# An RMS-norm kernel whose Tile context is closed after the first two loads, the rest in plain Bass

## The chip, the cores and the metric

The kernel runs on one core of one Trainium2 chip. The metric is the device time of one execution in microseconds (us). It is longer than the span, which reaches from the kernel's first instruction to its last: the difference holds what the runtime does behind the kernel. "Behind the span" means here the time minus the span. All runs quoted are at a granted clock of 1.0.

## The reference

```python
batch, seq, dim = 16, 1024, 512          # x is float32, gamma is all ones
rms = np.sqrt(np.mean(x ** 2, axis=-1, keepdims=True) + eps)
x_norm = x / rms * gamma
return np.maximum(x_norm, 0).astype(np.float32)
```

The input has 33.55 MB and so has the output; each is moved once.

## The kernel before

Each partition holds 16 rows of 512 numbers per chunk of 4 MB; eight chunks pass through six slots of SBUF. SyncE issues all loads and stores on one queue. ScalarE sums the squares of eight rows at a time and takes the root; VectorE inverts it, multiplies (by gamma too) and clips. GpSimd only waits for loads and passes them on as a count. The first chunk comes in two halves, so that compute starts early. All of it is traced inside a Tile context, in a critical section, with semaphores set by hand; the context adds its closing at the end.

```python
    ctx.enter_context(tc.manual_schedule(engines={mybir.EngineType.SP}))
    with tc.tile_critical():
        for m, (i, a, r) in enumerate(loads):        # loads of the first six chunks
            if i < nslots:
                load(m)                              # L77
        ...                                          # stores, the last two loads, and compute
    with nc.sync.register("landed") as landed:
        nc.sync.reg_mov(landed, 32)
        for s in range(nchunks - nslots, nslots):
            nc.sync.wait_ge(sem_slot[s], landed)
        nc.sync.reg_mov(landed, 64)
        for s in range(nchunks - nslots):
            nc.sync.wait_ge(sem_slot[s], landed)     # L171, the last wait
...
    with _tile.TileContext(nc) as tc:                # L202: on leaving it, Tile's closing
        tile_rmsnorm_relu_kernel(tc, *args)
```

## Time and profile before

| what | before |
|---|---|
| time, median of 4 runs | 162.28 us (162.23 to 162.32) |
| span of the profiled run | 160.37 us, its time 162.16 |
| transfers | first packet 1.95 us, last packet ends 158.84, last landing 159.32 |
| last wait passed | 159.34 us |
| Tile's closing | 159.40 to 160.37 us |
| behind the span | 162.16 - 160.37 = 1.79 us |

Read it in that order. The DMA row of the page, full to the last slice, says that the transfers bound the kernel. Everything that could be won is then ahead of the first packet or after the last one. The rows with L202 in the view of single source lines show the closing, which holds two barriers of all engines. The prediction below shows these lines.

### The profile page before, as it was taken

The numbers are of one execution on the slowest core, as the hardware profiler recorded it, in microseconds if no ns is written. First come the engines' busy times: TensorE is split into PE (matmuls) and PEld (weight loads), VectorE is DVE, ScalarE is ACT, GpSimd is POOL, SyncE is SP. The second block draws the span as 40 slices with busy tenths as digits, with TensorE's granted clock in tenths as the row PEclk, the third lists the DMA queues.
The fourth block names the chain that finished last, engine by engine and source line by source line (L and its number), as shares of the span: only waits on it lengthen the run. The fifth ranks groups of instructions, "written<-read, shape, count | busy, mean of one in ns | idle before, by whom it ended". The sixth has DMA issues, their size and how long they took to land. (4 is left out here: it accounts for less than half of the span.)

```text
span 160.4 us, 1008 instructions
## 1 busy us (share of the span) xinstructions
DVE 126.0 (79%) x164; ACT 86.3 (54%) x273; POOL 0.2 (0%) x4
## 2 busy tenths in 40 slices
DVE  1103989898989999999999999999999999995000
ACT  3088919889989988988910298899400000000000
POOL 0000000000000000000000000000000000000000
DMA  5999999999999999999999999999999999999993
GB/s 168 419 441 437 490 400 400 499 409 392 482 433 392 433 474 400 409 499 400 392 466 433 409 425 466 417 400 482 425 392 482 425 400 474 433 400 466 425 409 139
DMA packets 2456, 67.12 MB, mean 419 GB/s; under 512 B 276, under 2 KB 276, under 8 KB 280
## 3 DMA queue, kind: packets, MB, share of 16 engines
q1 hardware_dynamic: 2448, 67.11, 97.6%
q10 hardware_dynamic: 8, 0.01, 0.0%
HBM read 33.56 MB, written 33.55 MB: 419 GB/s over the span
## 5 line engine op out<-in xcount | busy, mean ns | idle before, releaser
L152 DVE SCALAR_TENSOR_TENSOR slots<-slots,rstd,gamma_sb 128x512 f32 x128 | 86.2, 747 | 4.8 <-DVEq L149 4.8
L128 ACT ACTIVATE junk<-slots 128x512 f32 x128 | 74.5, 582 | 22.2 <-ACTq L124 22.0
L163 DVE TENSOR_SCALAR slots<-slots x16 | 36.7, 2294 | 2.4 <-DVEq L162 0.2
L128 ACT ACTIVATION_READ_ACCUMULATOR junk<-slots x128 | 23.9, 187 | 0.0
L146 DVE RECIPROCAL rstd<-rms x16 | 3.2, 197 | 6.2 <-DVEq L142 6.2
L135 ACT ACTIVATE rms<-ss,eps_sb x16 | 4.8, 301 | 3.0 <-ACTq L134 3.0
L139 DVE LOAD_MASK_SELECT gamma_sb<-gseed x1 | 0.0, 14 | 6.0 <-DMA gseed<-in_gamma_dram 6.0
L120 ACT ACT_TABLE_LOAD x1 | 1.3, 1283 | 2.8 <-issue 2.8
L113 DVE MEMSET gseed<- 128x512 f32 x1 | 0.5, 485 | 1.1 <-SPq L93 1.1
L139 DVE STREAM_SHUFFLE gamma_sb<-gseed 128x512 f32<-128x512 f32 x1 | 0.7, 716 | 0.0
L188 POOL MEMSET const-bfloat16-1.0<- 128x1 bf16 x1 | 0.1, 102 | 0.0
L188 POOL MEMSET const-uint8-127<- 128x1 uint8 x1 | 0.1, 102 | 0.0
L188 POOL MEMSET const-float32-1.0<- 128x1 f32 x1 | 0.1, 99 | 0.0
L188 POOL MEMSET const-float32-0.0<- 128x1 f32 x1 | 0.1, 98 | 0.2 <-issue 0.2
L114 DVE MEMSET eps_sb<- 128x1 f32 x1 | 0.1, 59 | 0.0
## 6 DMA issues: line engine op xcount, KB each, us to landing
out_dram<-slots SPq DMA_DIRECT2D x8, 4096.0 KB, 20.7
slots<-in_x_dram SPq DMA_DIRECT2D x7, 4096.0 KB, 30.3
slots<-in_x_dram SPq DMA_DIRECT2D x2, 2048.0 KB, 9.6
gseed<-in_gamma_dram ACTq DMA_DIRECT2D x1, 8.0 KB
```

The costliest lines, as they stand in the source:

```text
L113: nc.vector.memset(gseed, 0.0).then_inc(sem_z, 1)
L114: nc.vector.memset(eps_sb, eps).then_inc(sem_z, 1)
L120: nc.scalar.preload_act_table(ACTF.Sqrt)
L128: a = nc.scalar.activation(out=junk[:, j, :], in_=slots[:, bass.ds(base + j * d, d)], func=ACTF.Square, accum_out=ss[:, bass.ds(col + j, 1)])
L135: nc.scalar.activation(out=rms[:, bass.ds(col, G)], in_=ss[:, bass.ds(col, G)], func=ACTF.Sqrt, bias=eps_sb, scale=inv_d).then_inc(sq, 1)
L139: nc.vector.stream_shuffle(gamma_sb, gseed, [0] * 32)
L146: nc.vector.reciprocal(out=rstd[:, bass.ds(col, G)], in_=rms[:, bass.ds(col, G)]).then_inc(sv, 1)
L152: r = nc.vector.scalar_tensor_tensor(out=row, in0=row, scalar=rstd[:, bass.ds(col + j, 1)], in1=gamma_sb, op0=ALU.mult, op1=ALU.mult)
L163: nc.vector.tensor_scalar_max(out=blk, in0=blk, scalar1=0.0).then_inc(done, 1)
L188: nc = _bacc.Bacc("TRN2", target_bir_lowering=False, num_devices=1)
```

## The change

The intent is to take Tile's closing out of the tail: Tile traces only the first two loads, is closed and compiled at once, and its closing barrier runs while these two transfer. All else follows as plain Bass. As Tile no longer clears the kernel's semaphores, each is brought back to zero by the engine that waits for it last.

```diff
-    with tc.tile_critical():
-        for m, (i, a, r) in enumerate(loads):
-            if i < nslots:
-                load(m)
+    early = 2
+    for m in range(early):
+        t = load(m)
+        tc.no_tile_sem_insts.add(t.ins.name)
+    ctx.close()
+    tc.close()
+    tc.compile()
+
+    for m, (i, a, r) in enumerate(loads):
+        if m >= early and i < nslots:
+            load(m)
     ...
+    def take(engine, sem, n):
+        engine.wait_ge(sem, n)
+        engine.sem_inc(sem, -n)
     ...
-    with nc.sync.register("landed") as landed:
-        nc.sync.reg_mov(landed, 32)
-        ...
+    take(nc.sync, done, ngroups)
+    take(nc.sync, tick1, ngroups)
+    take(nc.sync, tick3, ngroups)
+    for i in range(nchunks - nslots, nchunks):
+        take(nc.sync, sem_slot[i % nslots], 32 * (i // nslots + 1))
```

Cut from the diff: tensors and semaphores are now allocated from Bass instead of Tile, and the waits of the loops are written as takes. The loops themselves are the same.

More of the change, by code (lines that the diff above doesn't have):

```diff
@@ L40, with sbuf @@
     ov = out2.rearrange("(c p k) d -> c p k d", p=P, k=K)
-    singles = ctx.enter_context(tc.tile_pool(name="singles", bufs=1))
-    psum = ctx.enter_context(
-        tc.tile_pool(name="psum", bufs=1, space=bass.MemoryType.PSUM))
-    gseed = singles.tile([P, d], F32, name="gseed")
-    gamma_sb = singles.tile([P, d], F32, name="gamma_sb")
-    eps_sb = singles.tile([P, 1], F32, name="eps_sb")
-    ss = singles.tile([P, rows], F32, name="ss")
-    rms = singles.tile([P, rows], F32, name="rms")
-    rstd = singles.tile([P, rows], F32, name="rstd")
-    slots = singles.tile([P, nslots * K * d], F32, name="slots")
-    junk = psum.tile([P, G, d], F32, name="junk")
-    loads = [(0, 0, G), (0, G, K - G)] + [(i, 0, K) for i in range(1, nchunks)]
-    sem_half = tc.alloc_semaphore("half")
-    sem_slot = [tc.alloc_semaphore(f"slot{s}") for s in range(nslots)]
-    sem_g = tc.alloc_semaphore("gam")
-    sem_z = tc.alloc_semaphore("zero")
-    ready = tc.alloc_semaphore("ready")
-    sq = tc.alloc_semaphore("sq")
-    tick1 = tc.alloc_semaphore("tick1")
-    tick3 = tc.alloc_semaphore("tick3")
-    done = tc.alloc_semaphore("done")
-    sa = tc.alloc_semaphore("sa")
-    sv = tc.alloc_semaphore("sv")
+    def sbuf(name, shape):
+        return nc.alloc_sbuf_tensor(name, shape, F32).ap()
+    gseed = sbuf("gseed", [P, d])
+    gamma_sb = sbuf("gamma_sb", [P, d])
+    eps_sb = sbuf("eps_sb", [P, 1])
+    ss = sbuf("ss", [P, rows])
+    rms = sbuf("rms", [P, rows])
+    rstd = sbuf("rstd", [P, rows])
+    slots = sbuf("slots", [P, nslots * K * d])
+    junk = nc.alloc_psum_tensor("junk", [P, G, d], F32).ap()
+    loads = [(0, 0, G), (0, G, K - G)] + [(i, 0, K) for i in range(1, nchunks)]
+    sem_half = nc.alloc_semaphore("half")
+    sem_slot = [nc.alloc_semaphore(f"slot{s}") for s in range(nslots)]
+    sem_g = nc.alloc_semaphore("gam")
+    sem_z = nc.alloc_semaphore("zero")
+    ready = nc.alloc_semaphore("ready")
+    sq = nc.alloc_semaphore("sq")
+    tick1 = nc.alloc_semaphore("tick1")
+    tick3 = nc.alloc_semaphore("tick3")
+    done = nc.alloc_semaphore("done")
+    sa = nc.alloc_semaphore("sa")
+    sv = nc.alloc_semaphore("sv")
     def slot_ap(i):
@@ L76, in load @@
         i, a, r = loads[m]
-        nc.sync.dma_start(out=slot_ap(i)[:, a:a + r, :],
-                          in_=xv[i][:, a:a + r, :]
-                          ).then_inc(sem_half if m == 0 else sem_slot[i % nslots], 16)
-    def loaded(engine, m):
-        i = loads[m][0]
-        if m == 0:
-            engine.wait_ge(sem_half, 16)
-        else:
-            engine.wait_ge(sem_slot[i % nslots], 32 * (i // nslots) + 16)
+        return nc.sync.dma_start(out=slot_ap(i)[:, a:a + r, :],
+                                 in_=xv[i][:, a:a + r, :]
+                                 ).then_inc(sem_half if m == 0 else sem_slot[i % nslots], 16)
+    def take(engine, sem, n):
+        engine.wait_ge(sem, n)
+        engine.sem_inc(sem, -n)
     def store(i):
@@ L92 @@
     ctx.enter_context(tc.manual_schedule(engines={mybir.EngineType.SP}))
-    with tc.tile_critical():
-        for m, (i, a, r) in enumerate(loads):
-            if i < nslots:
-                load(m)
-        nc.sync.wait_ge(tick3, 6)
-        store(0)
-        store(1)
-        for s in range(2):
-            nc.sync.wait_ge(sem_slot[s], 32)
-            load(7 + s)
-        nc.sync.wait_ge(tick1, 11)
-        for i in range(2, nchunks):
-            store(i)
-        for m, (i, a, r) in enumerate(loads):
-            loaded(nc.gpsimd, m)
-            nc.gpsimd.sem_inc(ready, r // G)
-        nc.vector.memset(gseed, 0.0).then_inc(sem_z, 1)
-        nc.vector.memset(eps_sb, eps).then_inc(sem_z, 1)
-        nc.scalar.wait_ge(sem_z, 1)
-        nc.scalar.dma_start(out=gseed[0:P:32, :],
-                            in_=gamma[None, :].to_broadcast([P // 32, d])
-                            ).then_inc(sem_g, 16)
-        nc.scalar.preload_act_table(ACTF.Sqrt)
-        nc.scalar.wait_ge(sem_z, 2)
-        with nc.scalar.Fori(0, ngroups) as gi:
-            nc.scalar.wait_ge(ready, 1)
-            nc.scalar.sem_inc(ready, -1)
-            base = nc.scalar.snap((gi % (nslots * per)) * (G * d))
-            col = nc.scalar.snap(gi * G)
-            for j in range(G):
-                a = nc.scalar.activation(
-                    out=junk[:, j, :], in_=slots[:, bass.ds(base + j * d, d)],
-                    func=ACTF.Square, accum_out=ss[:, bass.ds(col + j, 1)])
-                if j == G - 1:
-                    a.then_inc(sa, 1)
-            nc.scalar.wait_ge(sa, 1)
-            nc.scalar.sem_inc(sa, -1)
-            nc.scalar.activation(out=rms[:, bass.ds(col, G)], in_=ss[:, bass.ds(col, G)],
-                                 func=ACTF.Sqrt, bias=eps_sb, scale=inv_d).then_inc(sq, 1)
-        nc.vector.wait_ge(sem_g, 16)
-        nc.vector.stream_shuffle(gamma_sb, gseed, [0] * 32)
-        with nc.vector.Fori(0, ngroups) as gi:
-            nc.vector.wait_ge(sq, 1)
-            nc.vector.sem_inc(sq, -1)
-            base = nc.vector.snap((gi % (nslots * per)) * (G * d))
-            col = nc.vector.snap(gi * G)
-            blk = slots[:, bass.ds(base, G * d)]
-            nc.vector.reciprocal(out=rstd[:, bass.ds(col, G)],
-                                 in_=rms[:, bass.ds(col, G)]).then_inc(sv, 1)
-            nc.vector.wait_ge(sv, 1)
-            nc.vector.sem_inc(sv, -1)
-            for j in range(G):
-                row = slots[:, bass.ds(base + j * d, d)]
-                r = nc.vector.scalar_tensor_tensor(
-                    out=row, in0=row, scalar=rstd[:, bass.ds(col + j, 1)], in1=gamma_sb,
-                    op0=ALU.mult, op1=ALU.mult)
-                if j == 0:
-                    r.then_inc(tick1, 1)
-                if j == 2:
-                    r.then_inc(tick3, 1)
-                if j == G - 1:
-                    r.then_inc(sv, 1)
-            nc.vector.wait_ge(sv, 1)
-            nc.vector.sem_inc(sv, -1)
-            nc.vector.tensor_scalar_max(out=blk, in0=blk, scalar1=0.0).then_inc(done, 1)
@@ L165 @@
-    with nc.sync.register("landed") as landed:
-        nc.sync.reg_mov(landed, 32)
-        for s in range(nchunks - nslots, nslots):
-            nc.sync.wait_ge(sem_slot[s], landed)
-        nc.sync.reg_mov(landed, 64)
-        for s in range(nchunks - nslots):
-            nc.sync.wait_ge(sem_slot[s], landed)
+    early = 2
[8 more added lines that the diff above has]
+            load(m)
@@ new lines @@
+    nc.sync.wait_ge(tick3, 6)
+    store(0)
+    store(1)
+    for s in range(2):
+        nc.sync.wait_ge(sem_slot[s], 32)
+        load(7 + s)
+    nc.sync.wait_ge(tick1, 11)
+    for i in range(2, nchunks):
+        store(i)
+    for m, (i, a, r) in enumerate(loads):
+        if m == 0:
+            take(nc.gpsimd, sem_half, 16)
+        else:
+            nc.gpsimd.wait_ge(sem_slot[i % nslots], 32 * (i // nslots) + 16)
+        nc.gpsimd.sem_inc(ready, r // G)
+    nc.vector.memset(gseed, 0.0).then_inc(sem_z, 1)
@@ new lines @@
+    nc.vector.memset(eps_sb, eps).then_inc(sem_z, 1)
+    nc.scalar.wait_ge(sem_z, 1)
+    nc.scalar.dma_start(out=gseed[0:P:32, :],
+                        in_=gamma[None, :].to_broadcast([P // 32, d])
+                        ).then_inc(sem_g, 16)
+    nc.scalar.preload_act_table(ACTF.Sqrt)
+    take(nc.scalar, sem_z, 2)
+    with nc.scalar.Fori(0, ngroups) as gi:
+        take(nc.scalar, ready, 1)
+        base = nc.scalar.snap((gi % (nslots * per)) * (G * d))
+        col = nc.scalar.snap(gi * G)
+        for j in range(G):
+            a = nc.scalar.activation(
+                out=junk[:, j, :], in_=slots[:, bass.ds(base + j * d, d)],
+                func=ACTF.Square, accum_out=ss[:, bass.ds(col + j, 1)])
+            if j == G - 1:
+                a.then_inc(sa, 1)
+        take(nc.scalar, sa, 1)
+        nc.scalar.activation(out=rms[:, bass.ds(col, G)], in_=ss[:, bass.ds(col, G)],
+                             func=ACTF.Sqrt, bias=eps_sb, scale=inv_d).then_inc(sq, 1)
@@ new lines @@
+    take(nc.vector, sem_g, 16)
+    nc.vector.stream_shuffle(gamma_sb, gseed, [0] * 32)
+    with nc.vector.Fori(0, ngroups) as gi:
+        take(nc.vector, sq, 1)
+        base = nc.vector.snap((gi % (nslots * per)) * (G * d))
+        col = nc.vector.snap(gi * G)
+        blk = slots[:, bass.ds(base, G * d)]
+        nc.vector.reciprocal(out=rstd[:, bass.ds(col, G)],
+                             in_=rms[:, bass.ds(col, G)]).then_inc(sv, 1)
+        take(nc.vector, sv, 1)
+        for j in range(G):
+            row = slots[:, bass.ds(base + j * d, d)]
+            r = nc.vector.scalar_tensor_tensor(
+                out=row, in0=row, scalar=rstd[:, bass.ds(col + j, 1)], in1=gamma_sb,
+                op0=ALU.mult, op1=ALU.mult)
+            if j == 0:
+                r.then_inc(tick1, 1)
+            if j == 2:
+                r.then_inc(tick3, 1)
+            if j == G - 1:
+                r.then_inc(sv, 1)
+        take(nc.vector, sv, 1)
+        nc.vector.tensor_scalar_max(out=blk, in0=blk, scalar1=0.0).then_inc(done, 1)
```

## The prediction

> **What bounds the kernel now.** I read the page first, then the DMA queue's own waits, the timeline of the last 30 us, the stretches at the end, and the single instructions by source line.
>
> The page says what is full:
>
> ```profile
> span 160.4 us, 1008 instructions
> DVE 126.0 (79%) x164; ACT 86.3 (54%) x273; POOL 0.2 (0%) x4
> DMA  5999999999999999999999999999999999999993
> ...
> q1 hardware_dynamic: 2448, 67.11, 97.6%
> ```
>
> No engine is full; the transfers are: one queue (q1) holds 16 engines for 97.6% of the span. The trace's packet records start at 1.95 us and end at 158.84 us, so 67.11 MB in 156.9 us, 428 GB/s without a hole. The kernel is therefore a head (before the first packet), a stream, and a tail (after the last packet). The chain view is of no help: it stops at VectorE's last operation at 144.2 us, as semaphore and DMA instructions are not counted as work.
>
> The waits of the DMA queue's own engine, SyncE, show what the end hangs on:
>
> ```profile
> SPq L77 <- DMA out_dram<-slots: 21.9, 2, 12.3
> SPq L171 <- DMA out_dram<-slots: 11.8, 1, 11.8
> ```
>
> L171 is the last wait of the kernel: SyncE stands there 11.8 us for the last stores. The stretches at the end and two source lines show what comes after it:
>
> ```profile
> 156.00:158.00 2.00, 0.00 (x0) 0.00 (x0) 0.00 (x0) 1.00 0.72 311
> 158.00:159.00 1.00, 0.00 (x0) 0.00 (x0) 0.00 (x0) 1.00 0.00 0
> 159.00:160.40 1.40, 0.00 (x0) 0.00 (x0) 0.00 (x0) 1.00 0.00 0
> ```
>
> ```profile
> L171 SPq EVENT_SEMAPHORE  x1: 17/17/17, 159.3 to 159.3; - x1
> ```
>
> ```profile
> L202 POOLq EVENT_SEMAPHORE  x4: 17/17/17, 159.6 to 160.3; - x4
> L202 SPq DRAIN  x3: 7/7/7, 159.5 to 159.9; - x3
> L202 SPq COMPARE_BRANCH  x2: 33/33/33, 0.8 to 159.4; - x2
> L202 POOLq EVENT_SEMAPHORE_RANGE_CLEAR  x1: 157/157/157, 159.9 to 159.9; - x1
> ```
>
> The columns of the stretches are length, busy time of three engines, clock, DMA share, GB/s. In the last stretch nothing moves. The source views (duration in ns, first and last start in us) say what runs there: the last wait passes at 159.34, then L202, the exit of Tile's context, runs a branch (159.40), a barrier of all engines (to 159.80), the clearing of Tile's range of semaphores (159.92, 157 ns) and a second barrier (160.19 to 160.37). That is 160.37 - 159.36 = **1.01 us** between the end of the last wait and the end of the span, on the path, with no work in it.
>
> **What the Trainium skill says.** (1) "DMA: Bandwidth & Descriptors", Specifications, gives a fabric ceiling of 435 GB/s for 16 engines. The trace agrees: 428 GB/s means that the stream has 2% left at most, and the change moves no byte. (2) "Perfetto Trace Analysis", Sequencer-only Instruction: the profiled window of such an instruction is its execution alone, the wait for a semaphore and its propagation are outside it. The trace agrees: the L171 entry lasts 17 ns but stood for 11.8 us. So I count the barrier by start times, not by durations. (3) "Runtime: NRT & Kernel Launch", The ~15us preamble/postamble breakdown: after the kernel the runtime makes a barrier over all engines, then resets semaphores. The trace agrees in kind: after the span a first series of nine updates of one semaphore runs from 160.61 to 161.13 us, the reset of all semaphores to 161.69, a second series from 161.92 to 162.27. The run timed 162.16 us against a span of 160.40, so about 1.8 us of the metric lies behind the span and is not the kernel's. (4) "DMA: Bandwidth & Descriptors", Queues, rings and completion order: each DMA engine takes turns between queues packet by packet, so gamma's small load has to queue beside the bulk. The trace agrees: gamma's issue ended at 2.73 us, its first packet began at 5.77 and it had landed at 7.54.
>
> **The change part by part.**
>
> *Removed at the end.* Tile's exit, its two barriers and the clearing no longer follow the last wait: -1.01 us, all of it on the path.
>
> *Added at the end.* SyncE takes the semaphores back to zero. A wait and its decrement ride on one instruction in the kernel before (ScalarE's wait on "ready" at 8.45 us has both), and those for done, tick1, tick3 and the first five slots are met while SyncE waits for the last store anyway: they become true up to 149.03 us, the last one at 159.32. Only the last slot's take is behind it, one instruction of 17 ns that stands where L171 stood, or two some 50 ns apart: **+0 to 0.06 us**.
>
> *Moved to the front.* The branch, both barriers and the clearing run after SyncE has issued the first two loads. SyncE's first issue starts at 0.94 us and the two take 0.387 and 0.425 us and end at 1.80. From the last branch to the last release (159.40 to 160.31) the sequence took 0.91 us. So SyncE starts load 2 near 2.75 us instead of 1.85, and the last of the five is issued near 5.0 instead of 4.1. The two early loads hold 4.19 MB; at 428 GB/s that is 9.8 us of stream from 1.95, until 11.8 us (the second lands at 13.2). The stream has 9 us of stock when load 2 comes, so the moved 0.91 us lie wholly **beside the stream: 0 us**.
>
> *Saved at the front.* Before, SyncE made a NOP (0.714 us) that opens the critical section, then a branch (0.784), then the first DMA. Without the section the NOP goes: the first issue moves by 0.784 - 0.714 = **-0.07 us**, and the whole stream with it.
>
> *Compute delayed at the front.* VectorE's memset (1.12 us before) and with it gamma's issue and ScalarE's table load (2.76 us) move by some 1.8 us: table load near 4.6, done near 5.9; ScalarE's first square starts at 8.78, set by the landing of the first half load at 8.38. Hidden by 2.5 us. Gamma lands near 7.54 + 1.8 = 9.4, shuffle of 716 ns done near 10.1; VectorE's first multiplication is at 15.03. Hidden by over 4 us.
>
> *GpSimd's first take* puts a decrement before the increment of ready: about 0.06 us on the first group. VectorE runs without a hole from 14.5 to 146.49 us and its last tick releases the last store, issued at 146.53. The previous store ends landing at 149.03, and from an issue to its first packet takes about 1.0 us (0.94 to 1.95 at the start). So VectorE's chain has about 149.03 - 146.53 - 1.0 = 1.5 us of slack, and 0.06 us vanish in it: **0 us**.
>
> *Behind the span.* Before, all five engines leave the last barrier together (160.33 to 160.37) and the runtime's first series shows one link of 0.205 us where the same link of the second series takes 0.039. One engine arrived late there by 0.17 us. After the change four engines are there long before and SyncE alone arrives last. That can save up to 0.17 us or nothing: **-0.1 us** as an estimate.
>
> *Left as it is.* The tensors have the same sizes[...], so neither the engines' modes nor the packets should change.
>
> Sum: 162.25 - 1.01 + 0.03 - 0.07 - 0.10 = **161.1 us**, a ratio of 0.993. The span alone: 160.40 - 1.05 = 159.35.
>
> **The rivals.**
>
> *Tile's closing waits for the two loads.* If the drain, or a wait that Tile adds for the loads, held SyncE until both had landed (13.2 us), then load 2 would be issued at 14.1 and its first packet come at 15.1, while the stream ran dry near 12.8: +2.3 us, time about 163.4. For it: a closing barrier exists to wait for what is open. Against it: the change lists both loads as instructions without Tile's semaphores, and a drain alone does not wait for transfers: SyncE's drain at 146.98 us (the critical section's exit) took 0.053 us with two stores in flight.
>
> *The end is paid elsewhere.* If the runtime's own barrier behind the kernel has a fixed cost from the last arrival that Tile's barrier partly hid (an engine that halts, is restarted or fetches the runtime's code only then), the 1.0 us shrinks. For it: the gap from the span's end to the first update behind it, 0.24 us, is hidden code of each engine. Against it: that code comes after the last instruction of either kernel. Time: 161.3 to 161.7.
>
> *A bonus at the front.* If the branch into the block goes too, or is fetched sooner, the first DMA starts 0.15 us or more earlier. For it: SyncE's branch costs 0.16 us up to the next instruction. Against it: a Tile context still opens a block. Time: 160.9.
>
> *The first packets collide otherwise.* Gamma's packets come at 7 to 9 us instead of 6 to 7, in the same stream: no byte more. Not seen as a cost.
>
> **Range and chances.** The main term (1.0 us) is a plain difference of start times, and the three runs of before lie within 0.09 us. What is unsure is the end behind the span (0 to 0.2 us less, perhaps 0.2 more), the front (0 to 0.15 us less) and whether the take is longer than thought. That gives 160.7 to 161.5. Faster by over 2% would need 159.0, which only a faster stream could give: 0.01. Slower by over 2% needs 165.5, more than the first rival costs: 0.01. Within 2%: 0.98.
>
> **What would show it right or wrong.** Right: the span is 159.2 to 159.5; the last instruction is SyncE's take of the last slot, within 0.1 us after the last landing; the barriers and the clearing stand between 1.7 and 2.8 us; the third to seventh loads are issued from about 2.7 to 5.0 us and no slice of the DMA row after the first falls below 9 before the last; the packets still take 156.9 us; gamma is shuffled near 9.4 us and VectorE's first reciprocal stays at 14.5. Wrong: a hole in the DMA row around 12 to 15 us (first rival), a gap from span to time that grows from 1.8 us (second), a first issue earlier than 0.8 us (third), or a stream whose length changed by more than 0.2 us, which none of these steps explains.

## The result

The changed kernel took **160.61 us** (median of 4 runs, 160.44 to 160.68) against 162.28 (162.23 to 162.32). The ratio is 0.9896 with a 95% interval of 0.9878 to 0.9913. Ratios here divide the mean time of one kernel's runs by that of the other's of the same rounds, so they are not quite the ratios of the medians quoted. By the 2% rule this is the same time; the difference is nevertheless clear of the scatter. The gain is larger than predicted, and the time lies 0.09 us below the stated range.

The page after, in its lines that answer to those of before:

```profile
span 159.3 us, 999 instructions
DVE 126.0 (79%) x164; ACT 86.3 (54%) x273; POOL 0.2 (0%) x4
DMA  6999999999999999999999999999999999999995
...
q1 hardware_dynamic: 2448, 67.11, 98.2%
```

The busy times of the engines are the same to the tenth. The transfers fill a larger share of a shorter span, and there is no hole in the DMA row.

SyncE's own waits after (L83 is the line of the helper `take`, L98 that of Tile's compile), and the last two stretches, whose columns are those of the prediction's:

```profile
SPq L83 <- SPq L83: 12.0, 2, 9.7
SPq L98 <- PEq L98: 0.4, 2, 0.3
```

```profile
158.00:159.00 1.00, 0.00 (x0) 0.00 (x0) 0.00 (x0) 1.00 0.00 0
159.00:159.30 0.30, 0.00 (x0) 0.00 (x0) 0.00 (x0) 1.00 0.00 0
```

Of the 1.40 us after 159 us, 0.3 is left. The single instructions of the two lines say why:

```profile
L83 SPq EVENT_SEMAPHORE  x9: 17/17/17, 146.9 to 159.2; - x9
```

```profile
L98 POOLq EVENT_SEMAPHORE  x4: 17/17/17, 1.9 to 2.3; - x4
L98 SPq DRAIN  x3: 7/7/128, 1.6 to 2.1; - x3
L98 SPq EVENT_SEMAPHORE  x2: 17/17/17, 2.0 to 2.3; - x2
```

The last of SyncE's nine takes starts at 159.245 us, lasts 17 ns and ends the span at 159.262. The closing stands at 1.64 to 2.36 us, and SyncE's part of it ends at 2.31. It holds no clearing of a range any more; the semaphores are now allocated from Bass.

The start of the transfers, the line L77 (issue of loads; first and last start in us after the three durations), before and then after:

```profile
L77 SPq DMA_DIRECT2D slots<-in_x_dram x9: 340/425/723, 0.9 to 81.5; - x9
```

```profile
L77 SPq DMA_DIRECT2D slots<-in_x_dram x9: 328/426/676, 0.7 to 81.2; - x9
```

To three digits the first issue moved from 0.941 to 0.731 us. Compute at the start, from the timeline (start, length, engine, line, what), before and then after:

```profile
1.12 0.48 DVE L113 MEMSET gseed<- 128x512 f32 x1 [1.12 <-SPq L93]
...
2.76 1.28 ACT L120 ACT_TABLE_LOAD   x1 [2.76 <-issue]
...
8.78 0.60 ACT L128 ACTIVATE junk<-slots 128x512 f32 x1 [4.74 <-ACTq L124]
...
14.53 0.20 DVE L146 RECIPROCAL rstd<-rms  x1 [6.24 <-DVEq L142]
```

```profile
2.55 0.48 DVE L122 MEMSET gseed<- 128x512 f32 x1 [2.55 <-PEq L98]
...
4.18 1.28 ACT L129 ACT_TABLE_LOAD   x1 [4.18 <-issue]
...
8.73 0.60 ACT L136 ACTIVATE junk<-slots 128x512 f32 x1 [3.27 <-ACTq L83]
...
14.48 0.20 DVE L152 RECIPROCAL rstd<-rms  x1 [5.30 <-DVEq L83]
```

The setting up waits for the closing and comes 1.4 us later; the first square and the first reciprocal, which depend on the first landing, come 0.05 us earlier. (The first half load landed 0.12 us earlier, at 8.26 instead of 8.38; GpSimd's take in front of its count uses up 0.07 us of that.)

The account of the two profiled runs, whose times differ by 162.16 - 160.59 = 1.57 us:

| stretch | before | after | difference |
|---|---|---|---|
| span's start to first packet | 1.952 | 1.748 | -0.20 |
| first packet to end of last packet | 156.891 | 157.003 | +0.11 |
| last packet to last take or wait | 0.495 | 0.494 | 0.00 |
| from that one's start to the span's end | 1.033 | 0.017 | -1.02 |
| behind the span | 1.79 | 1.33 | -0.46 |

The last row was predicted at -0.10 and the first at -0.07. The trace records the runtime's work behind the span as updates of one semaphore. Before, a first series of nine comes at 160.606, 160.640, 160.845, 160.890, 160.913, 161.011, 161.050, 161.085 and 161.131 us. After, four of the nine are long done (2.595, 114.155, 114.193 and 146.593 us), and only five come after the span's end at 159.262: 159.394, 159.438, 159.476, 159.510 and 159.557. From the span's end to the ninth update it was 0.760 us before and is 0.295 after: 0.465 us less, the whole of the last row. What follows is the same in all thirteen profiles: a second series of nine begins 0.79 us after the ninth update, and its last update comes 0.11 to 0.12 us after the span's start plus the time of that run. So the time ends at a fixed distance behind the ninth update.

### The profile page after: what moved, and what is told of

Read it like the earlier page. It is cut to its first block, busy times and chain, and to the rows that moved or that the text cites. A ratio compares the mean times of both kernels' runs of the same rounds, so it can differ in the third digit from the quotient of the medians.

```text
span 159.3 us, 999 instructions
## 1 busy us (share of the span) xinstructions
DVE 126.0 (79%) x164; ACT 86.3 (54%) x273; POOL 0.2 (0%) x4
```

## The experiments

**Theory A**, formed from these records: the runtime's first series is a chain through the engines and back (TensorE, ScalarE, GpSimd, VectorE, SyncE, and the same way back to TensorE). An engine adds its update when it has finished and its turn has come. So what is paid behind the span is the delay of the last engine's own update plus the updates that follow it. The four early updates fit the engines' last work: TensorE after the closing (2.3 us), ScalarE near 114, GpSimd right after it since it had finished before, VectorE near 146.5. SyncE is then the fifth of nine, at the turn. **Theory B**: the saving has nothing to do with who is last; the kernel just no longer ends with Tile's barriers and clearing. **Theory F**, on the front: a NOP and a branch that stood ahead of SyncE's first issue are both gone, and the 0.2 us reach the end. All edits are to the changed kernel.

### The unedited changed kernel on the same chip

> The changed kernel, nothing edited, as the yardstick on this chip. Both theories: about 160.6 us, span about 159.3, and 1.3 us from the span's end to the end of the timed run (before: 1.8).

It took 160.83 us (160.55 to 160.99; before, in the same rounds, 162.38), ratio 0.9897 (0.9877 to 0.9917). Mean span 159.47, and on average 1.33 us behind the span against 1.78 for the kernel before: as expected, while the time is 0.2 us above what was expected. Its profiled run had a stream of 157.37 us, 0.37 more than the profile of the same kernel shown above; more on this below.

### Another engine last

```diff
     for i in range(nchunks - nslots, nchunks):
-        take(nc.sync, sem_slot[i % nslots], 32 * (i // nslots + 1))
+        last = nc.tensor if i == nchunks - 1 else nc.sync
+        take(last, sem_slot[i % nslots], 32 * (i // nslots + 1))
```

and the same with `nc.gpsimd` and `nc.vector`. These edits make the kernel slower on purpose; the results stay correct.

> The last slot's take is done by TensorE, SyncE has ended before. Theory A (what is paid behind the span depends on the place that the last engine has in the runtime's series of nine updates, TensorE first, then ScalarE, GpSimd, VectorE, SyncE and back): TensorE opens the series, so all nine updates come after it; 0.235 us to the first and 0.356 for the other eight, from the trace of before, 0.59 against 0.295 us with SyncE: time about 160.9, span as the control, behind the span about 1.63. Theory B (the saving behind the span comes from the kernel no longer ending in a barrier with a clearing, whoever is last): as the control, 160.6 and 1.33.

> The last slot's take is done by GpSimd. Theory A: GpSimd's update came 0.56 us after its last instruction in the trace of before, and six more follow in 0.286 us, so 0.85 us against 0.295: time about 161.15, behind the span about 1.88, span as the control. Theory B: as the control, 160.6 and 1.33.

> The last slot's take is done by VectorE, fourth in the runtime's series. Theory A: six updates from its own on come after it, 0.24 us without its own delay, and its own delay lies between SyncE's 0.13 and TensorE's 0.28 us, so 0.37 to 0.52 us from the last instruction to the ninth update, against 0.29 with SyncE and 0.64 with TensorE: behind the span about 1.45, time about 160.85. Theory B: 1.33 behind the span as with SyncE.

The line of `take` (L83) in the three profiles shows the last take where the edit put it; TensorE, GpSimd and VectorE last, in this order:

```profile
L83 PEldq EVENT_SEMAPHORE  x1: 51/51/51, 159.4 to 159.4; - x1
```

```profile
L83 POOLq EVENT_SEMAPHORE  x2: 17/17/17, 8.1 to 159.3; - x2
```

```profile
L83 DVEq EVENT_SEMAPHORE  x50: 21/21/21, 8.2 to 159.3; - x50
```

The times were 161.09 us (TensorE), 161.22 (GpSimd) and 160.90 (VectorE). The spans did not change with them (means of 159.38, 159.30 and 159.47), what is behind did. The table in the next section has all of it. Theory A had expected 1.63, 1.88 and 1.45 us behind the span; measured were means of 1.69, 1.89 and 1.45. Theory B, 1.33 for all, falls.

### A barrier at the end again

```diff
         take(nc.sync, sem_slot[i % nslots], 32 * (i // nslots + 1))
+    nc.all_engine_barrier()
```

> The changed kernel with one barrier of all engines put back at the end, without the clearing and the second barrier. Theory A: the span grows by one barrier, 0.25 to 0.45 us, to about 159.65, and behind it stand 1.8 us again as all engines leave together with GpSimd late: time about 161.4. Theory B: span the same 159.65, behind it 1.33 as nothing is cleared: time about 161.0.

```profile
L174 POOLq EVENT_SEMAPHORE  x2: 17/17/17, 159.7 to 159.8; - x2
...
L174 SPq DRAIN  x1: 7/7/7, 159.6 to 159.6; - x1
...
L174 PEldq EVENT_SEMAPHORE  x1: 51/51/51, 159.8 to 159.8; - x1
```

It took 161.40 us (161.34 to 161.65). The barrier itself cost 0.287 us of span (from the start of the last take at 159.575 to the end at 159.862), and behind the span stand 1.78 us again, the value of before, though nothing is cleared and there is only one barrier. So one barrier at the end costs twice: in the span, and behind it as it lets the engines finish together. Together they cost 0.65 us (means of 161.45 against 160.80), less than half of what the change had gained.

The table for all placements; the two columns of the profiled run are from the end of the last instruction to that engine's update, and from there to the ninth update (SyncE: the unedited changed kernel of this section; VectorE ran in other rounds):

| last to finish | own update | to the ninth | sum | mean behind the span |
|---|---|---|---|---|
| all together (before) | | | 0.760 | 1.78 |
| all together (barrier) | | | 0.759 | 1.78 |
| GpSimd, 3rd | 0.561 | 0.292 | 0.853 | 1.89 |
| TensorE, 1st | 0.279 | 0.365 | 0.644 | 1.69 |
| VectorE, 4th | 0.188 | 0.242 | 0.430 | 1.45 |
| SyncE, 5th | 0.131 | 0.163 | 0.294 | 1.33 |

The last column minus the sum is 1.02 to 1.05 us in every row, and 1.02 to 1.03 if the profiled run's own time behind the span is taken in place of the mean. So the rest of what is behind the span is constant. The place alone does not set the cost: GpSimd is dearer than TensorE, which comes before it, because its own update takes longer. Why that takes 0.13 us on one engine and 0.56 on another was not examined. ScalarE as the last was not run; its place, second, is inferred from its early update near 114 us.

### The critical section round the two early loads

```diff
-    for m in range(early):
-        t = load(m)
-        tc.no_tile_sem_insts.add(t.ins.name)
+    with tc.tile_critical():
+        for m in range(early):
+            load(m)
```

> The two early loads stand in a critical section of Tile again, as all did before; all else as changed. Theory F (the first issue came 0.21 us earlier because a NOP and a branch stood ahead of it on SyncE, not only the NOP): the first issue moves from 0.73 back to about 0.94 us and the first packet from 1.75 to about 1.95; time about 160.8 to 161.0, behind the span 1.3 as the changed kernel. Rival (only the NOP, 0.07 us, as was predicted, and the rest chance): first issue near 0.80, first packet near 1.82, time about 160.7.

```profile
L77 SPq DMA_DIRECT2D slots<-in_x_dram x9: 327/426/674, 0.9 to 81.5; - x9
```

The trace has SyncE's NOP at 0.712 us, the branch at 0.782, the first issue at 0.935 and the first packet at 1.947: the head of the kernel before, in all its parts. The rival's 0.80 us falls. It took 161.01 us. Whether the 0.2 us reach the end was still open, as the control of other rounds lay 0.2 to 0.4 us below, so both ran again together:

> The changed kernel again, as the yardstick for the two below in the same rounds: about 160.7 to 160.8 us, first packet at 1.75 us.

> The critical section round the two early loads again, now in the same rounds as the control. Theory F: the first packet comes 0.20 us later and this reaches the end: the mean time is 0.12 to 0.28 us above the control's. Rival (the gain at the first packet is lost in the stream, as the profiled pair of before and after suggests, 0.20 us at the first packet but 0.09 at the last): 0 to 0.1 us above the control.

The control took 160.63 us (160.51 to 160.82) and the critical section 160.95 (160.84 to 161.06); the means of four runs each are 160.65 and 160.95. The difference, 0.30 us, is just above what theory F had named and well above its rival's. The intervals of the two ratios still overlap (0.9874 to 0.9907 against 0.9890 to 0.9923). The record has a second check. Between the kernel before and the changed one, the means differ by 1.69, 1.62 and 1.77 us in the three sets of rounds; the tail and what is behind the span took 1.48 us of it in the profiles, which leaves 0.14 to 0.29 us for the front and the stream together. If the profiled tail holds for all runs, the gain at the front reaches the end in the main.

The landings tell more. A transfer is finished by sixteen separate increments, and the trace has each. For the last store the first increment landed at 158.01, 157.95 and 157.98 us in three profiles of the changed kernel, and at 158.28 and 158.23 with the critical section (before: 158.21). So most of the stream did keep the 0.2 us. The last increment, which ends the kernel, lags: it came 0.69 to 1.23 us after the fifteenth in the three profiles of the changed kernel, 0.51 and 0.79 with the critical section, and 0.52 in the one of before. This is the +0.11 of the account above. In these three profiles it is the scatter too: the first increments lie within 0.06 us of each other, the last came at 159.23, 159.59 and 159.30. That it also makes the spans of the runs without a profile go from 159.1 to 159.7 us is not shown. The lag grows with the stores: in the first profile of the changed kernel the sixteen increments of the third store lie within 0.74 us and those of the last within 1.22, while those of each of the first seven loads stay within 0.75 us in all three profiles. Why one of sixteen lags was not examined.

### No early load, and seven of them

```diff
-    early = 2
+    early = 0
```

and `early = 7`.

> No load is traced ahead of the closing: both barriers and the clearing are then on the path before the first packet. Theory (a stock of early loads hides the moved closing): the first issue comes at about 1.45 instead of 0.73 us, the stream moves by 0.7 us, time about 161.3 to 161.5, span about 160.1. Rival (the front was never what counted, the end alone does): 160.6 to 160.8.

> All seven first loads are issued ahead of the closing, so VectorE's memset, gamma and the table load come some 2.7 us later still: memset near 5.2, gamma landed near 11, shuffled before 12. The step says that compute has 2.5 us (ScalarE) and more (VectorE) in hand: time as the control, 160.6 to 160.9, first square within 0.3 us of 8.73 and VectorE's first reciprocal within 0.3 of 14.5. Rival (compute's start is on the path): 162 or more.

> All seven first loads ahead of the closing, in the same rounds as the control. Hidden either way: within 0.1 us of the control. Rival (the later issue of the third to seventh load costs the changed kernel something): 0.1 to 0.3 us below the control.

With none, from the timeline:

```profile
1.38 2.59 SPq L77 DMA_DIRECT2D slots<-in_x_dram  x5
```

The first issue comes 0.65 us later than the changed kernel's 0.73, the first packet at 2.40, and the time was 161.46 us (161.38 to 161.68; means of the runs 161.50 here and 160.68 over the twelve unedited, all of other rounds, as these held no unedited changed kernel). So the closing costs about as much at the front as it lasts, if nothing covers it: 0.65 us at the first issue, 0.8 in the time, whose scatter is some tenths. With all seven loads ahead:

```profile
5.16 0.48 DVE L122 MEMSET gseed<- 128x512 f32 x1 [5.16 <-PEq L98]
...
6.79 1.28 ACT L129 ACT_TABLE_LOAD   x1 [6.79 <-issue]
8.55 0.60 ACT L136 ACTIVATE junk<-slots 128x512 f32 x1 [0.48 <-ACTq L83]
```

The table load now ends at 8.07 us and the first square, at 8.55, is still set by the first landing. The time was 160.70 us (160.59 to 160.80), 0.1 below the control of the rounds before, and in the second set of rounds 160.91 (160.70 to 161.00), 0.23 us above its control by the means. The two disagree in sign and are within the scatter, so nothing is shown either way beyond a tenth or two; ScalarE's setting up has 3.27 us to spare at two loads (its idle time before the first square, shown above), and 0.48 us at seven. No experiment beat the changed kernel clearly; of the four engines tried, it already ends on the cheapest.

What was not run: the two loads with Tile's own semaphores on them. It does not build: Tile stops with the message that the kernel's own semaphore update is all that the instruction accepts.

## Why the prediction was wrong

- **Right: the tail.** 1.01 us were predicted to leave the path at the end, and the stretch from the start of the last wait to the span's end fell from 1.033 to 0.017 us. The last take costs 17 ns where the wait before cost 17 ns, so the 0.03 us put down for it are nil.
- **Wrong, and the step that failed: "Behind the span".** The prediction estimated -0.1 us and named 0.17 as the most there is. The record shows -0.46. It had the right mechanism in view (one engine alone arrives last) but took from it only the lateness of one link, the 0.205 us that should be 0.039. It did not see that the series is a chain with an order, so that every update ahead of the last engine's leaves the path too, and that the engine which made the link late (GpSimd, 0.56 us from its last instruction to its update) no longer counts at all. It also read all five engines as leaving together (160.33 to 160.37): GpSimd had left first, at 160.284, so its update was late by its own delay and not by its arrival. With SyncE last, four of nine updates are done, and 0.131 + 0.163 us remain of 0.760. The three other placements, 0.43 to 0.85 us where SyncE has 0.29, and the barrier that brought back 1.78 us behind the span show this. The range allowed 0 to 0.2 us here. This term at its measured size puts the sum at 160.74, still inside the stated range; it took the next one too to leave it.
- **Too small: "Saved at the front".** -0.07 us was predicted for a NOP, -0.21 was measured at the first issue, as the branch went too. The third rival, a bonus at the front of 0.15 us more, described this; it was left out of the sum. The critical section put back shows both parts by name.
- **Right in kind, off in size: "Moved to the front".** It lies beside the stream: without an early load the time rises by 0.8 us, with two it does not. The closing is shorter than thought, 0.66 us from the first drain (1.641) to SyncE's release (2.297) instead of 0.91, and neither a branch nor the clearing moved along. Load 2 is issued at 2.37 us, not 2.75.
- **Right: compute is hidden.** Gamma landed at 8.28 us and its shuffle came at 8.45, not at 9.4. The shorter closing explains 0.4 us of that (the setting up moved by 1.43 us, not 1.8); the rest is a shorter way from issue to landing, 5.2 us against 5.9 before, which was not examined. The first reciprocal stayed (14.53 to 14.48). Even 2.6 us more, with seven early loads, left the first square where the landing put it. One line was misread without harm: the store in front of the last one had fully landed at 149.65 us, not 149.03 (the thirteenth of its sixteen increments), so VectorE's slack is 0.6 us more than the 1.5 named.
- **Fallen rivals.** Tile's closing does not wait for the loads: SyncE's longest drain there took 128 ns, and load 2 was issued at 2.37 us, long before the first landing at 7.70. The end is not paid elsewhere either: what is behind the span shrank.
- **Left to chance by the stream.** It was predicted to last 156.9 us; profiles of the changed kernel show 157.00 to 157.37, and the lagging increment follows the last packet by 0.48 us in each.

With the measured terms the sum is 162.28 - 1.02 - 0.46 - 0.21 = 160.59 us, against 160.61 measured. That it fits to 0.02 us is luck: the 0.11 us by which the stream was longer in the profiled run is left out, and the stream scatters by some tenths.

## What to carry to other kernels

Where transfers fill the time, look at the microsecond after the last landing and ask of each instruction there whether it could run at the start, under the first transfers. Then let one engine alone finish last, and choose it by measuring: here the end was cheapest on SyncE, 0.14 us dearer on VectorE, 0.35 on TensorE, 0.56 on GpSimd, and a closing barrier took back all that was gained behind the span, and 0.29 us of span besides. Read the stretch behind the span as part of the kernel's time, since what the kernel's last instructions look like decides part of it.

## What the Trainium skill lacked or had wrong

- "Runtime: NRT & Kernel Launch", The ~15µs preamble/postamble breakdown, gives one figure for the barrier behind a kernel, about 1.5 us. Here, from the kernel's last instruction to the ninth update of the first series, it took 0.29 us with SyncE last, 0.43 with VectorE, 0.64 with TensorE, 0.85 with GpSimd and 0.76 with all together; that the cost depends on who finishes last is not on the page. For the barrier in front of a kernel the page has a chain that winds over five engines in some 355 ns, at 44 ns a step. The second series behind this kernel fits it: nine updates in 0.356 us (161.917 to 162.273), with single steps of 0.02 to 0.10 us. The prediction drew on this section and did not use the chain.
- The same place gives about 1.5 us for the reset of semaphores behind the kernel. In the trace of before their updates run from 161.03 to 161.69 us, 0.66 us, and 0.61 us after the change.
- "DMA: Bandwidth & Descriptors", Latency and other measured facts, says that two of the sixteen DMA engines are usually slower than the rest in traces, without a size, and holds this to be specific to transfers that GpSimd issues. Here SyncE issued all of the large transfers, and one of the sixteen increments of the last store came 0.5 to 1.2 us after the fifteenth, differing between executions of one kernel, and set the end. The kept trace does not tell which engine it was.
